# Attention scores and attention output: three fp32r passes in place of plain fp32 matmuls

## The chip, the cores and the metric

The kernel runs on one core of one Trainium2 chip. The number that counts is the device time of one execution in microseconds (us), as the median of several runs. A profiled execution shows what the core's engines did: PE (TensorE, matmuls; PEld is its loading of the stationary operand), DVE (VectorE), ACT (ScalarE), POOL (GpSimd) and SP (SyncE, which issues the DMAs).

## What is computed

One layer with two branches that read the same normalised input: an mLSTM branch and a latent attention branch (MLA). The change lies in the attention branch. There are 512 prompt tokens, and 64 new tokens of a second stream that has 128 cached keys; 8 heads, keys of 128 unrotated and 64 rotated columns, values of 128 columns.

```python
def mla_attend(qn, qr, q_pos, kn, kr, v, k_pos):
    s = (jnp.einsum('bqhd,bkhd->bhqk', qn, kn) + jnp.einsum('bqhd,bkd->bhqk', qr, kr)).astype(jnp.float32) * ATT_SCALE
    mask = (k_pos[None, :] // CHUNK) <= (q_pos[:, None] // CHUNK)
    s = jnp.where(mask[None, None], s, NEG)
    p = jax.nn.softmax(s, axis=-1).astype(v.dtype)
    return jnp.einsum('bhqk,bkhd->bqhd', p, v)
...
    q_nope = rmsnorm(q[..., :NOPE], g_qn)
    k_nope = rmsnorm(kv[..., :NOPE], g_kn)
    v = kv[..., NOPE:]
```

CHUNK is 64, so in a block of 128 queries that meets its own 128 keys, the first 64 queries may not see the last 64 keys. Everything is fp32.

## The kernel before

**Split products.** Most products in this kernel are made as three passes in the type fp32r: each operand is split into a rounded part (hi) and the rest (lo), and hi·hi, hi·lo and lo·hi are added up in PSUM. `split_of` makes the parts: a copy to hi on ACT, a subtraction for lo on DVE. `gemm_f` and `gemm_t` issue such products; `fblock` makes one 128-column block of an input projection for all 576 tokens (48 matmuls of 288 columns), with its weights loaded and split by `wload`.

**The attention stage** runs two heads (a pair) at a time. Its steps stand in the string `PLAN`: `K` makes queries, keys and values of a pair, `H` does one head, `Z` is the `fblock` of a head's gate, `G` the `fblock` of a merge gate that is needed at the end of the program (it is sent to DRAM), `P` the output projection of a pair. The stages follow one another as "G0 K0 Z0 H0 Z1 K1 H1 G2 G1 Z2 P0 H2 Z3 Z4 H3 ...".

- `K` (in `kq`): six `k_tile`s and five `q_tile`s, as generators, so that a tile's second half is issued after the first half of the second tile behind it. A `k_tile` makes 128 tokens' keys and values in PSUM, copies the keys to `kn` (DVE) and the values to `v` (ACT), takes the norm (ACT squares, DVE, POOL power of -0.5), scales `kn` on DVE, transposes it on PE and writes `kT` by ACT. A `q_tile` does alike for queries, with the rotation of the 64 rotary columns on POOL (lines 461 to 464).
- `H` (in `head`): scores of four query blocks against 128, 256, 384 and 512 keys and of the 64 sample tokens against 192. The unrotated part is a plain fp32 matmul (lines 529 and 536), the rotated part two fp32r matmuls (531, 538). The mask is a fourth matmul of one row, `indrow` by `negrow` (532), which adds -1e30 where a key is not to be seen. `soft` then takes maximum (510), exponential (511), reciprocal and scale. The probabilities are transposed on PE (547), copied to `pT` (548), and multiplied with `v` in plain fp32 (559, and 562, 563 for the sample tokens). The result multiplies the gate `za` (561, 564), and `split_of` makes the two parts `ha`.

A plain fp32 matmul shows in the trace as two MATMUL records.

**Buffers.** PSUM has three pools: `mm` with two banks (an `fblock` takes both), `sa` with three (scores, transposed probabilities, head outputs) and `sk` with three (K's tiles). In SBUF `qT` and `kT` have four buffers each, that is two pairs; `v` has two for pairs; the gate `za` has two; the tile `tg` of a `G` has one of its own.

**What sets the order.** The program is written in the order of `PLAN`. A scheduler then fixes, when the program is built, one order for each engine's queue: it goes by the order of the text, but takes a later instruction where an earlier one isn't ready by its own estimate, as long as a buffer is free for it. On the chip each engine works its queue off in that order and waits where an operand or a buffer is late.

Of the kernel before, what the change touches and what calls it, by code (L numbers as in the profile page):

```python
# [6 lines left out]
F32 = mybir.dt.float32  # L7
# [6 lines left out]
P = 128  # L14
# [13 lines left out]
# order in which the work of the first two stages is issued (see `steps` and the attention loop)  # L28
# [9 lines left out]
def layer(ctx: ExitStack, tc, A, O):  # L38
# [37 lines left out]
    negrow = const.tile([1, 64], BF16, name="negrow")  # L76
    dve.memset(negrow, NEG)
    indrow = const.tile([1, P], BF16, name="indrow")
    dve.memset(indrow, 0.0)
    dve.memset(indrow[:, 0:64], 1.0)  # L80
# [26 lines left out]
    def wload(srcs, nk, n, wp=None, unit=1024):  # L107
# [7 lines left out]
        hi = shp(wp.tile([P, unit], F32R, tag="whi", name="whi", bufs=2))  # L115
        lo = shp(wp.tile([P, unit], F32R, tag="wlo", name="wlo", bufs=2))
# [15 lines left out]
    def gemm_s(out, ws, x, t0):  # L132
        # 64 tokens: both parts of x, side by side in memory, are one stationary operand; fold() adds the results
# [54 lines left out]
    with ExitStack() as es:  # L188
# [151 lines left out]
        def gates():  # L340
            # log-sigmoid, running sums and maxima; rows are (chunk, head)
# [87 lines left out]
    with ExitStack() as es:  # L429
# [6 lines left out]
        def q_tile(wq, n, qT, qrT):  # L436
# [469 lines left out]
```

## Time and profile before

| | us |
|---|---|
| median of 3 runs | 825.41 |
| lowest, highest | 824.75, 825.55 |
| span of the profiled execution, first to last instruction | 822.5 |
| PE busy in the span | 810.0 |
| DVE busy | 478.7 |
| ACT busy | 362.0 |
| POOL busy | 141.4 |

The attention stage lies at about 60 to 370 us, the start ahead of it, the mLSTM heads and the output projection behind it. A busy time is the time in which an engine had some instruction under way. Matmuls overlap: the distance from one matmul's start to the next says what it costs the engine, and the duration of one record is longer than that.

### The profile page before, as it was taken

The page shows a single profiled execution, that of the slowest core. Times are in us where ns is not written, and L with a number is a line of the kernel's source. Part 1 is how long each engine was busy: PE and PEld are TensorE (multiplying, and loading weights), DVE is VectorE, ACT ScalarE, POOL GpSimd, SP SyncE. Part 2 cuts the span into 40 slices and gives each one's busy share as a digit, 9 for nine tenths or more (in the row PEclk, how much of TensorE's full clock was granted, in tenths as well). Part 3 has the DMA queues.
Part 4 walks back from the last instruction along what each step waited for, and adds up shares of the span by engine and source line. Part 5 has one row for each costly group of instructions (what it writes and reads, how often), then busy time and mean ns, then how long its engine had stood idle before and what let it go on. Part 6 is the DMA issues. An engine that isn't in the chain of part 4 may idle for free.

```text
span 822.5 us, 14924 instructions
## 1 busy us (share of the span) xinstructions
PE 810.0 (98%) x5759; PEld 761.5 (93%) x5759; DVE 478.7 (58%) x1211; ACT 362.0 (44%) x999; POOL 141.4 (17%) x253
## 2 busy tenths in 40 slices
PE   7899999999999999999999999999999999999998
PEld 6898997888898798889999999999999999999997
DVE  5666566755576658545534873775477355655431
ACT  5446556663555654322434544444454434332200
POOL 2343241410143133001001110110111011000000
PEclk9999999999999999999999999999999999999999
DMA  8431231013113011126223232333333432543332
GB/s 267 138 108 59 74 111 27 1 52 106 41 52 120 27 41 33 46 84 157 78 77 91 66 106 74 103 84 97 91 94 96 118 87 68 165 124 106 101 95 76
DMA packets 101742, 72.80 MB, mean 89 GB/s; under 512 B 5742, under 2 KB 95848, under 8 KB 101672
## 3 DMA queue, kind: packets, MB, share of 16 engines
q1 hardware_dynamic: 101672, 71.86, 30.5%
q8 instruction: 45, 0.74, 0.4%
q14 instruction: 25, 0.20, 0.1%
HBM read 64.24 MB, written 7.61 MB: 87 GB/s over the span
## 4 chain that ended last, share of the span: by engine, by line
PE 94%; DMA 3%; DVE 1%; ACT 1%; issue 0%; SPq 0%; POOL 0%; DVEq 0%; ACTq 0%
PE mm L126 58%; PE sk L143 10%; PE sk L852 3%; PE sa L852 3%; PE sa L529 2%; PE sa L728 2%; PE sa L559 2%; PE sk L728 2%; PE sk L136 2%; PE sa L531 1%; PE sa L547 1%; PE sk L745 1%; PE sa L136 1%; PE sk L502 1%; DMA part<-in_w_in 1%; DMA E<-gscr 1%
## 5 line engine op out<-in xcount | busy, mean ns | idle before, releaser
L105 DVE TENSOR_TENSOR wlo<-raw,whi 128x1024 fp32r<-128x1024 f32 (+1 forms) x88 | 108.5, 1234 | 92.1 <-ACT whi L104 87.1
L104 ACT CAST whi<-raw 128x1024 fp32r<-128x1024 f32 (+1 forms) x88 | 92.6, 1055 | 135.2 <-PE mm L126 91.9
L126 PE MATMUL mm<-hhi,whi 128*128 128x288 f32 x896 | 147.1, 300 | 1.1 <-ACT hhi L104 1.1
L126 PE MATMUL mm<-hhi,wlo 128*128 128x288 f32 x896 | 146.6, 299 | 0.0
L126 PE MATMUL mm<-hlo,whi 128*128 128x288 f32 x896 | 145.7, 298 | 0.0
L126 PEld LDWEIGHTS mm<-hhi,whi 128*128 128x128 f32 x896 | 126.6, 188 | 2.1 <-ACT hhi L104 1.4
L126 PEld LDWEIGHTS mm<-hlo,whi 128*128 128x128 f32 x896 | 127.1, 188 | 1.3 <-issue 0.5
L126 PEld LDWEIGHTS mm<-hhi,wlo 128*128 128x128 f32 x896 | 126.9, 188 | 1.2 <-issue 0.5
L74 POOL TENSOR_TENSOR r<-r,mhalf 128x2 f32<-128x2 f32 (+3 forms) x44 | 37.2, 844 | 165.4 <-DVE r L495 109.4
L126 PE MATMUL mm<-ha,whi 128*128 128x288 f32 x256 | 48.2, 307 | 0.6 <-DVE part L595 0.6
L126 PEld LDWEIGHTS mm<-ha,whi 128*128 128x128 f32 x256 | 37.3, 188 | 2.7 <-DVE part L595 1.1
L511 ACT ACTIVATE P<-sa,sc 128x128 f32<-128x128 f32 (+4 forms) x40 | 20.1, 503 | 36.4 <-DVE sc L510 35.6
L752 POOL TENSOR_TENSOR qi<-qf,wi 128x256 f32<-128x256 f32 (+1 forms) x16 | 11.9, 744 | 105.7 <-ACT qf L710 54.3
L595 DVE TENSOR_TENSOR part<-part,mm 128x288 f32<-128x288 f32 x48 | 21.4, 452 | 11.8 <-PE mm L126 11.6
L74 POOL TENSOR_TENSOR sc<-sc,mhalf 128x1 f32<-128x1 f32 (+1 forms) x20 | 13.0, 648 | 87.0 <-DVE sc L784 87.0
L126 PE MATMUL mm<-ha,wlo 128*128 128x288 f32 x128 | 27.5, 296 | 0.0
L105 POOL TENSOR_TENSOR qi<-qi,qi 128x256 fp32r<-128x256 f32 (+1 forms) x16 | 10.7, 668 | 85.3 <-ACT qi L104 85.3
L529 PE MATMUL sa<-kT,qT 128*128 128x128 f32 (+3 forms) x64 | 23.4, 447 | 0.0
L510 DVE TENSOR_REDUCE sc<-sa 128x1 f32<-128x128 f32 (+4 forms) x40 | 18.3, 457 | 8.5 <-PE sa L532 6.4
L728 PE MATMUL sk<-va,kw 128*128 128x258 f32 (+1 forms) x120 | 22.2, 290 | 0.1
L823 DVE SCALAR_TENSOR_TENSOR mt<-tgm,mm 128x288 f32<-128x288 f32 x16 | 7.3, 454 | 25.1 <-PE mm L126 25.1
L474 ACT ACTIVATE qT<-sk,gqn_c 128x128 f32<-128x128 f32 (+1 forms) x40 | 12.2, 354 | 18.8 <-PE sk L472 18.8
(353 smaller groups left out, 1641.0 us busy)
## 6 DMA issues: line engine op xcount, KB each, us to landing
raw<-in_w_in SPq DMA_DIRECT2D x56, 512.0 KB, 3.8
raw<-in_w_pa SPq DMA_DIRECT2D x8, 512.0 KB
raw<-in_w_pm SPq DMA_DIRECT2D x8, 512.0 KB, 4.2
raw<-in_w_uq SPq DMA_DIRECT2D x4, 576.0 KB, 4.0
gmscr<-tg SPq DMA_DIRECT2D x8, 288.0 KB
tgm<-gmscr SPq DMA_DIRECT2D x8, 288.0 KB, 4.3
xt<-in_x_prompt SPq DMA_DIRECT2D x4, 512.0 KB, 6.7
raw<-in_w_ukv SPq DMA_DIRECT2D x4, 512.0 KB, 3.8
```

What stands on the lines that cost most here:

```text
L74: pool.tensor_tensor(dst, ms, mhalf[0:n, 0:dst.shape[-1]], op=ALU.pow)
L104: act.copy(hi, src)
L105: (eng or dve).tensor_tensor(lo, src, hi.bitcast(F32), op=ALU.subtract)
L126: pe.matmul(ps[j], a[:, k0 + k, c0:c0 + P], b[:, k, sl], start=(n == 0), stop=(n == len(trip) - 1))
L136: pe.matmul(out, x[:, k, t0:t0 + P], a, start=(i == 0), stop=(i == len(trip) - 1))
L143: pe.matmul(out, b[:, k, t0:t0 + L], a[:, k, c0:c0 + n], start=(i == 0), stop=(i == len(trip) - 1))
L510: dve.tensor_reduce(sc[0:L, 0:1], ps, AX.X, ALU.max, negate=True)
L511: act.activation(pt[0:L, 0:n], ps, AF.Exp, bias=sc[0:L, 0:1], accum_out=sc[0:L, 1:2])
L529: pe.matmul(ps[:, 0:n], qT[hh][:, q0:q0 + P], kT[hh][:, 0:n], start=True, stop=False)
L595: dve.tensor_tensor(part[:, f, sl], part[:, f, sl], ps[j], op=ALU.add)
L728: pe.matmul(out, x, y, start=(first and i == 0), stop=(last and i == 2))
L852: pe.matmul(ps[0:L, 0:NB], x[:, 4 * u + k, t0:t0 + L], w[u][i][:, k], start=(q == 0), stop=(q == len(trip) - 1))
```

## The change

The scores' unrotated part and both products with `v` become three fp32r passes on split operands. For that queries, keys, values and transposed probabilities are stored as hi and lo parts: `scaled_split` scales from PSUM to hi on ACT and writes lo by one DVE operation. The mask matmul goes; a DVE memset writes -1e30 to 64 rows and 64 columns of the scores in PSUM. In `k_tile` the copy to `kn` goes: squares and scale (now on ACT) read PSUM, which is thus held until the scale is done. Buffers are per head, three for each of `qT`, `qrT`, `kT` and `v` (hi and lo), and the tile `tg` of a `G` now takes one of the two buffers of `za`. In `head` the output's PSUM bank `of` is taken ahead of the transposes, and the products with `v` follow each block of transposes rather than all of them. The scratch space of dynamic DMAs is set to 1024 bytes.

```diff
-    def wload(srcs, nk, n, wp=None, unit=1024):
+    def wload(srcs, nk, n, wp=None, unit=1024, tag="", bufs=2):
...
-                act.activation(qT[hh][:, t0:t0 + L], ps2[:, hh * P:hh * P + L], AF.Copy, scale=gqn_c)
-            dve.tensor_copy(qrT[:, :, t0:t0 + L], ps2.rearrange("p (k t) -> p k t", k=4)[:, 2:4, 0:L])
+                scaled_split(qT[hh], t0, L, ps2[:, hh * P:hh * P + L], gqn_c)
+                dve.tensor_copy(qrT[hh][:, t0:t0 + L], ps2[:, (2 + hh) * P:(2 + hh) * P + L])
...
+        def scaled_split(dst, t0, L, src, g):
+            hi, lo = (x[:, t0:t0 + L] for x in dst)
+            act.activation(hi, src, AF.Copy, scale=g)
+            dve.scalar_tensor_tensor(lo, src, g, hi.bitcast(F32), ALU.mult, ALU.subtract)
...
-                dve.tensor_copy(kn, pv[:, :, 0:NOPE])
-                act.copy(v[:, n], pv[:, :, NOPE:])
...
+            for hh in range(2):
+                split_of(v[hh][0:L, 0, n], v[hh][0:L, 1, n], pv[0:L, hh, NOPE:])
...
-                act.activation(sq[0:L], kn[0:L, hh], AF.Square, scale=NOPE ** -0.5, accum_out=r2[0:L, hh:hh + 1])
+                act.activation(sq[0:L], pv[0:L, hh, 0:NOPE], AF.Square, scale=NOPE ** -0.5, accum_out=r2[0:L, hh:hh + 1])
...
-                dve.tensor_scalar(kn[0:L, hh], kn[0:L, hh], r2[0:L, hh:hh + 1], None, ALU.mult)
+                act.activation(kn[0:L, hh], pv[0:L, hh, 0:NOPE], AF.Copy, scale=r2[0:L, hh:hh + 1])
...
-                act.activation(kT[hh][:, t0:t0 + L], ps2[:, hh * P:hh * P + L], AF.Copy, scale=gkn_c)
+                scaled_split(kT[hh], t0, L, ps2[:, hh * P:hh * P + L], gkn_c)
...
+        def scores(out, hh, qT, qrT, kT, qc, kc):
+            (qh, ql), (kh, kl) = qT[hh], kT[hh]
+            pairs = [(qh, kh), (qh, kl), (ql, kh), (qrT[hh], krhi), (qrT[hh], krlo)]
+            for i, (a, b) in enumerate(pairs):
+                pe.matmul(out, a[:, qc], b[:, kc], start=(i == 0), stop=(i == 4))
...
-                pe.matmul(ps[:, 0:n], qT[hh][:, q0:q0 + P], kT[hh][:, 0:n], start=True, stop=False)
-                for kr in (krhi, krlo):
-                    pe.matmul(ps[:, 0:n], qrT[:, hh, q0:q0 + P], kr[:, 0:n], start=False, stop=False)
-                pe.matmul(ps[:, n - 64:n], indrow, negrow, start=False, stop=True)
+                scores(ps[:, 0:n], hh, qT, qrT, kT, slice(q0, q0 + P), slice(0, n))
+                dve.memset(ps[0:64, n - 64:n], NEG)
...
+            of = SA()
...
-                (act.copy if j % 2 else dve.tensor_copy)(pT[:, o:o + w], ps[:, 0:w])
-                off.append(o)
-                o += w
+                pT = [aq.tile([P, 4 * P], F32R, tag=f"pT{x}", name=f"pT{x}", bufs=2)[:, 0:w] for x in range(2)]
+                split_of(pT[0], pT[1], ps[:, 0:w])
+                for i, (x, y) in enumerate(((0, 0), (0, 1), (1, 0))):
+                    pe.matmul(of[:, j * P:SEQ], v[:, x, j], pT[y], start=(j == 0 and i == 0), stop=(j == 3 and i == 2))
+            dve.tensor_tensor(za[:, 0:SEQ], of, za[:, 0:SEQ], op=ALU.mult)
...
-            qT = [aq.tile([P, T], F32, tag="qT", name="qT", bufs=4) for _ in range(2)]
-            qrT = aq.tile([P, 2, T], F32R, tag="qrT", name="qrT", bufs=2)
-            kT = [ak.tile([P, TK], F32, tag="kT", name="kT", bufs=4) for _ in range(2)]
-            v = ak.tile([P, 6, 2, VD], F32, tag="v", name="v", bufs=2)
...
+            qT = [[aq.tile([P, T], F32R, tag=f"qT{i}", name=f"qT{i}", bufs=3) for i in range(2)] for _ in range(2)]
+            qrT = [aq.tile([P, T], F32R, tag="qrT", name="qrT", bufs=3) for _ in range(2)]
+            kT = [[ak.tile([P, TK], F32R, tag=f"kT{i}", name=f"kT{i}", bufs=3) for i in range(2)] for _ in range(2)]
+            v = [ak.tile([P, 2, 6, VD], F32R, tag="v", name="v", bufs=3) for _ in range(2)]
...
-                gm_block(i, aq.tile([P, T], F32, tag="tg", name="tg", bufs=1))
+                gm_block(i, aq.tile([P, T], F32, tag="za", name="tg", bufs=2))
...
-    nc = _bacc.Bacc("TRN2", target_bir_lowering=False, num_devices=1)
+    nc = _bacc.Bacc("TRN2", target_bir_lowering=False, num_devices=1, dynamic_dma_scratch_size=1024)
```

How this moves instructions is seen at two places. A row names line, operation, output and inputs, and size; a number behind a name tells buffers of one name apart.

On ACT, during the first head (H0): L173 reads the results of the `fblock`s of G2 and G1 out of `mm`, and the rows of P_1404 and P_1415 are H0's first exponentials. Before:

```order
L511 ACTIVATE P_1404,sc<-sa,sc 128x128
L450 ACTIVATE sq,r_1252<-qs 128x128
L451 ACTIVATE sq,r_1252<-qs 128x64
L173 ACTIVATE tg<-mm 128x288
L511 ACTIVATE P_1415,sc<-sa,sc 128x256
L474 ACTIVATE qT<-sk,gqn_c 128x128 x2
L104 CAST whi<-raw 128x1024
L450 ACTIVATE sq,r_1291<-qs 64x128
L173 ACTIVATE tg<-mm 128x288
```

After, the first read of `mm` by a `tg` that follows G0's stands behind H0's last step, the split of `za` into `ha_1438`, and among the exponentials of the second head (P_2039 and on):

```order
L512 ACTIVATE P_2039,sc<-sa,sc 128x128
L99 CAST v<-sk 128x128 x3
L512 ACTIVATE P_2052,sc<-sa,sc 128x256
L99 CAST ha_1438<-za 128x576
L495 ACTIVATE sq,r_1663<-sk 128x128
L512 ACTIVATE P_2065,sc<-sa,sc 128x384
L495 ACTIVATE sq,r_1663<-sk 128x128
L495 ACTIVATE sq,r_1683<-sk 128x128
L168 ACTIVATE tg<-mm 128x288 x2
```

The read of G2's block has moved from H0's scores to a place behind H0.

On PE, in the third head (H2): transposes of the probabilities P (L547, after L549), `fblock` matmuls (L126) and the products with `v` (L559, after L553). Before:

```order
L547 MATMUL sa<-ident,P_2349 128x128
L547 MATMUL sa<-ident,P_2360 128x128 x2
L126 MATMUL mm<-hhi,wlo 128x288 x3
L552 MATMUL sa<-ident,P_2370 128x64
L553 MATMUL sa<-ident,P_2370 64x64
L126 MATMUL mm<-hhi,wlo 128x288 x3
L126 MATMUL mm<-hhi,whi 128x288 x8
L126 MATMUL mm<-hlo,whi 128x288 x8
L126 MATMUL mm<-hhi,wlo 128x288 x2
L559 MATMUL sa<-pT,v 128x512
L559 MATMUL sa<-pT,v 128x384
L559 MATMUL sa<-pT,v 128x256
```

After (pT_2551, pT_2562 are hi parts, pT_2552, pT_2563 lo parts):

```order
L549 MATMUL sa<-ident,P_2501 128x128
L549 MATMUL sa<-ident,P_2514 128x128
L549 MATMUL sa<-ident,P_2527 128x128
L553 MATMUL sa<-pT_2552,v 128x512
L553 MATMUL sa<-pT_2551,v 128x512
L549 MATMUL sa<-ident,P_2514 128x128
L549 MATMUL sa<-ident,P_2527 128x128
L553 MATMUL sa<-pT_2562,v 128x384
L553 MATMUL sa<-pT_2563,v 128x384
L553 MATMUL sa<-pT_2562,v 128x384
L553 MATMUL sa<-pT_2572,v 128x256
```

The `fblock` matmuls between transposes and products are gone from here; the products follow two transposes behind the block that they need.

## Rows read from the trace of the kernel before

**Rows 1.** The page: span, engines' busy time, and the granted PE clock by slices.

```profile
span 822.5 us, 14924 instructions
PE 810.0 (98%) x5759; PEld 761.5 (93%) x5759; DVE 478.7 (58%) x1211; ACT 362.0 (44%) x999; POOL 141.4 (17%) x253
...
PEclk9999999999999999999999999999999999999999
```

**Rows 2.** PE's longest wait: waited for, us in total, times, longest us.

```profile
PE sa L267 <- DVE xs L262: 2.7, 2, 1.4
```

**Rows 3.** Busy us (x instructions) of PE, PEld, DVE, ACT, POOL, clock; the attention stage.

```profile
60.00:370.00 310.00, 309.41 (x1954) 269.56 (x1954) 196.56 (x589) 162.19 (x582) 76.58 (x138) 1.00 0.20 58
```

**Rows 4.** The same for PE and PEld, L126 alone, in the first head.

```profile
104.00:125.00 21.00, 14.55 (x89) 12.02 (x87) 1.00 0.33 104
```

**Rows 5.** Timeline of PE between two heads: start us, us, engine, line, tiles, shapes.

```profile
276.37 2.42 PE L559 MATMUL sa<-pT,v 128*128 128x512 f32 x8
278.63 0.39 PE L529 MATMUL sa<-kT,qT 128*128 128x128 f32 x2
...
280.46 0.33 PE L562 MATMUL sa<-pTs,v 128*128 128x64 f32 x2
280.73 0.43 PE L563 MATMUL sa<-pTs,v 64*128 64x64 f32 x2
...
281.74 0.28 PE L531 MATMUL sa<-krlo,qrT 128*128 128x256 f32 x1
281.96 0.20 PE L532 MATMUL sa<-negrow,indrow 1*128 1x64 bf16 x1
...
285.09 0.20 PE L532 MATMUL sa<-negrow,indrow 1*128 1x64 bf16 x1
285.22 0.79 PE L143 MATMUL sk<-whi,cqhi 128*128 128x384 f32 x3
285.85 0.68 PE L143 MATMUL sk<-whi,cqlo 128*128 128x384 f32 x3
286.37 0.69 PE L143 MATMUL sk<-wlo,cqhi 128*128 128x384 f32 x3
```

**Rows 6.** The same timeline, two fp32r passes of 512 columns each.

```profile
263.49 0.62 PE L143 MATMUL sk<-whi,cklo 128*128 128x512 f32 x2
263.95 0.62 PE L143 MATMUL sk<-wlo,ckhi 128*128 128x512 f32 x2
```

**Rows 7.** Groups of PE instructions: xcount, busy us, mean ns, idle us: the mask matmuls.

```profile
L532 PE MATMUL sa<-negrow,indrow 1*128 1x64 bf16 x32 | 6.3, 198 | 0.0
```

**Rows 8.** Timeline of POOL: query tiles of the first pair, second to fifth.

```profile
100.59 1.01 POOL L74 TENSOR_TENSOR r<-r,mhalf 128x4 f32<-128x4 f32 x1 [3.95 <-DVE r L452]
...
110.57 1.01 POOL L74 TENSOR_TENSOR r<-r,mhalf 128x4 f32<-128x4 f32 x1 [0.48 <-DVE r L452]
...
113.47 0.46 POOL L464 TENSOR_TENSOR qr<-qr,rt 128x128 f32<-128x128 f32 x1
117.26 1.00 POOL L74 TENSOR_TENSOR r<-r,mhalf 64x4 f32<-64x4 f32 x1 [3.33 <-DVE r L452]
```

**Rows 9.** Groups of DVE and ACT instructions around the heads, as in rows 7.

```profile
L561 DVE TENSOR_TENSOR za<-sa,za 128x512 f32<-128x512 f32 x8 | 5.5, 690 | 10.0 <-PE sa L559 9.9
L510 DVE TENSOR_REDUCE sc<-sa 128x1 f32<-128x512 f32 x8 | 5.5, 687 | 5.0 <-PE sa L532 4.8
...
L513 DVE TENSOR_SCALAR P<-P,sc 128x384 f32<-128x384 f32 x8 | 3.3, 412 | 0.1
...
L510 DVE TENSOR_REDUCE sc<-sa 64x1 f32<-64x192 f32 x8 | 2.7, 343 | 1.7 <-PE sa L538 1.5
...
L564 DVE TENSOR_TENSOR za<-sa,za 128x64 f32<-128x64 f32 x8 | 1.7, 218 | 0.4 <-PE sa L563 0.4
...
L641 DVE MEMSET xp<- 128x3 f32 x8 | 0.5, 61 | 0.0
...
L511 ACT ACTIVATE P<-sa,sc 128x512 f32<-128x512 f32 x8 | 5.5, 688 | 14.1 <-DVE sc L510 14.1
```

More of the change, by code (lines that the diff above doesn't have):

```diff
@@ L74, in rsqrt_of @@
         pool.tensor_tensor(dst, ms, mhalf[0:n, 0:dst.shape[-1]], op=ALU.pow)
[L76 to L80, printed above, removed]
     cols = const.tile([P, 82], F32, name="cols")
@@ L114, in wload @@
             o += s.shape[0] // P
-        hi = shp(wp.tile([P, unit], F32R, tag="whi", name="whi", bufs=2))
-        lo = shp(wp.tile([P, unit], F32R, tag="wlo", name="wlo", bufs=2))
+        hi = shp(wp.tile([P, unit], F32R, tag="whi" + tag, name="whi", bufs=bufs))
+        lo = shp(wp.tile([P, unit], F32R, tag="wlo" + tag, name="wlo", bufs=bufs))
         split_of(hi, lo, raw)
@@ L522, in z_block @@
             return za
+        def scores(out, hh, qT, qrT, kT, qc, kc):
[3 more added lines that the diff above has]
+                pe.matmul(out, a[:, qc], b[:, kc], start=(i == 0), stop=(i == 4))
         def head(hh, qT, qrT, kT, v, za, ha):
+            v = v[hh]
             pts = []
@@ L535, in head @@
             nk = PAST + DEC
-            pe.matmul(ps[0:DEC, 0:nk], qT[hh][:, SEQ:T], kT[hh][:, SEQ:TK], start=True, stop=False)
-            for kr in (krhi, krlo):
-                pe.matmul(ps[0:DEC, 0:nk], qrT[:, hh, SEQ:T], kr[:, SEQ:TK], start=False, stop=(kr is krlo))
+            scores(ps[0:DEC, 0:nk], hh, qT, qrT, kT, slice(SEQ, T), slice(SEQ, TK))
             pt = soft(ps[0:DEC, 0:nk], DEC, nk)
-            pT = aq.tile([P, 10 * P], F32, tag="pT", name="pT", bufs=1)
-            off = []
-            o = 0
+            of = SA()
             for j in range(4):
@@ L553, in head @@
             pe.transpose(ps[0:DEC, 64:64 + DEC], pt[0:DEC, P:nk], ident[0:DEC, 0:DEC])
-            pTs = aq.tile([P, 2, DEC], F32, tag="pTs", name="pTs", bufs=1)
-            act.copy(pTs[:, 0], ps[:, 0:DEC])
-            act.copy(pTs[0:DEC, 1], ps[0:DEC, 64:64 + DEC])
-            of = SA()
-            for j in range(4):
-                pe.matmul(of[:, j * P:SEQ], v[:, j, hh], pT[:, off[j]:off[j] + (4 - j) * P],
-                          start=(j == 0), stop=(j == 3))
-            dve.tensor_tensor(za[:, 0:SEQ], of, za[:, 0:SEQ], op=ALU.mult)
-            pe.matmul(ps[:, 128:128 + DEC], v[:, 4, hh], pTs[:, 0], start=True, stop=False)
-            pe.matmul(ps[:, 128:128 + DEC], v[0:DEC, 5, hh], pTs[0:DEC, 1], start=False, stop=True)
+            pTs = [aq.tile([P, 2, DEC], F32R, tag=f"pTs{x}", name=f"pTs{x}", bufs=1) for x in range(2)]
+            split_of(pTs[0][:, 0], pTs[1][:, 0], ps[:, 0:DEC])
+            split_of(pTs[0][0:DEC, 1], pTs[1][0:DEC, 1], ps[0:DEC, 64:64 + DEC])
+            for c, L in ((0, P), (1, DEC)):
+                for i, (x, y) in enumerate(((0, 0), (0, 1), (1, 0))):
+                    pe.matmul(ps[:, 128:128 + DEC], v[0:L, x, 4 + c], pTs[y][0:L, c], start=(c == 0 and i == 0), stop=(c == 1 and i == 2))
             dve.tensor_tensor(za[:, SEQ:T], ps[:, 128:128 + DEC], za[:, SEQ:T], op=ALU.mult)
```

11 lines of the change are left out of this document (6 added, 5 removed).

## The prediction, made before the changed kernel ran

> **What bounds the kernel now.** I read the page's line of engines first: PE is busy for 810.0 of 822.5 us, the next engine, DVE, for 478.7, and PE's granted clock is at its upper level in every slice [rows 1]. Then the waits: PE's longest group of waits is 2.7 us in all, in one line of the start [rows 2]. Then the stretch in which everything that changes lies, 60 to 370 us: PE is busy in 309.41 of 310 us there, DVE in 196.56, ACT in 162.19, POOL in 76.58 [rows 3]. So PE sets the time and never waits in the attention stage; the other engines have room. The change is worth what it takes out of PE's queue, less the waits that it brings to PE. The median, 825.4, is 2.9 us above the span; I add that to what I reckon for the span.
>
> **The price of a pass.** Matmuls overlap, so I take the distance between starts. Two fp32r passes of 512 columns take 263.49 to 263.95, that is 0.23 us each [rows 6]; three of 384 take 285.85 to 286.37, 0.173 each [rows 5]. Both are 0.45 ns per column. The plain product with `v` has 1280 columns in four widths, two records for each, and takes 276.37 to 278.63, 2.26 us [rows 5], 0.88 ns per column and record, 1.77 for a product. Three passes cost 1.35 ns per column, a quarter less, as long as the columns set the price. For few columns they don't: two records of 64 columns take 280.46 to 280.73, 0.135 each, and the mask matmul of 64 columns takes 285.09 to 285.22, 0.13 [rows 5]. For a pass of 256 I take 0.12 (0.45 ns a column gives 0.115) and for one of 128 I take 0.11, near the short ones; its ends are 0.058 (by columns) and 0.135.
>
> **The change, part by part.**
>
> The mask matmul goes, 32 of them [rows 7]. Each costs its own 0.13. It also slows its neighbours: the 256-column pass ahead of it takes 281.74 to 281.96, 0.22 in place of 0.12, and the three 384-column passes behind another take 285.22 to 285.85, 0.63 in place of 0.52 [rows 5]. Together 0.13 + 0.10 + 0.10 = 0.33, times 32: **-10.6 us**. The end of that is -4.2 if the neighbours' part stays.
>
> The product with `v`: three passes cost 3 x (0.23 + 0.173 + 0.12 + 0.11) = 1.90 in place of 2.26, so -0.36 a head, **-2.8**. The scores' unrotated part has the same four widths and the same sum, **-2.8**; the 192 columns of the sample tokens come out even (0.33 against 0.34). The sample product with `v` goes from two records to three passes, twice: two such pairs take 0.27 + 0.36 = 0.63 [rows 5], so a third more is +0.21 a head, **+1.7**. With a 128-column pass at its ends the three together move between -6.4 and -2.7.
>
> PE's queue thus gets shorter by 10.6 + 2.8 + 2.8 - 1.7 = **14.5 us**, and nothing that hides another engine's work can take this back but a wait of PE.
>
> Waits of PE, and here the order counts more than the prices. Before, every chain of a head (maximum, exponential, scale, transpose, copy, product) ran beside `fblock` matmuls. In the first head these filled 14.55 of 21 us [rows 4]. After, `tg` needs a buffer of `za`, so G2's `fblock` cannot empty `mm` before H0 has given up its gate, and the second example of the order ahead shows the same in H2: the transposes and products stand back to back. Buffers of `qT`, `kT` and `v` for three heads, not four, hold the next pair's tiles back too.
>
> First head. Between the transposes of K0's second query tile and those of its fifth, the order after leaves PE 15 passes of 384, 12 of 512, some 19 transposes and the first head's scores: 2.6 + 2.8 + 2.1 + 3.2 = 10.7 us. The tiles' chain took 117.26 - 100.59 = 16.7 us in POOL's records before, with waits of POOL for DVE of 3 to 4 us among them [rows 8]. POOL's own part is at least 3.4 us a tile (110.57 to 113.93), 10 us for three. So PE waits between 0 and 6 us. I take 6, because the waits in that chain were for DVE, and DVE gets more to do: lo parts for queries, keys, values and probabilities.
>
> Heads with a dense stretch (H0 with H1's scores, H2 with H3's, H4 with H5's). Three places. The lo pass of the second block needs transposes, ACT's cast and DVE's subtraction (about half a microsecond each for 384 columns, by the 0.69 that 512 cost [rows 9]) and has 0.85 us of PE work between: wait 0.4. The second scores of the next head need the bank of `of`, which is free after DVE's multiplication, 0.69 [rows 9], with 0.55 of PE work between: 0.4 with the hand-over. The third transpose of the next head needs the 384-column probabilities, whose scale stands on DVE behind the maxima of the 512 and the 192 columns: from the end of the 512 scores 0.1 + 0.69 + 0.34 + 0.41 [rows 9] and four hand-overs, against 0.8 us of PE work (sample scores, two transposes): 1.4 with a tenth or two for each hand-over. With 0.3 for the rest it is 2.5 a stretch, 7.5 in all. H6 with H7's scores has some fill left, 1.3; the last head's products have little behind them, 1.2. Sum of the waits: 6 + 7.5 + 2.5 = **+16 us**; the ends are 6 (half of each, and nothing at the first head) and 24 (each stretch half as dear again).
>
> What DVE and ACT get on top: 32 memsets, each between 0.06 (a memset of 128x3) and 0.22 (a 128x64 operation with PSUM) [rows 9], I take 0.1 as it writes only; the second parts, 88 of them for queries and keys, at 0.3 to 0.5 us. That is some 30 us on DVE in a stage that leaves it 113 free [rows 3]; elsewhere PE's work covers it. If it didn't, that is the second rival. Three constants less at the start, single buffers for K's weights and the smaller DMA scratch: nothing, the weights are loaded a whole stage ahead, and PE's waits of the start are elsewhere [rows 2].
>
> A rule to be weighed against the pass prices: the Trainium skill, "TensorE: Matmul & The Clock Gate", section "Back-to-back issue gap", gives 131 ns per matmul of 512 columns in a stream and 81 ns for 128. This trace has 230 ns for 512 [rows 6], so I don't take it; by it a head's two sets of three passes would be about 1.25 us shorter (an estimate from that section's two figures), 10 in all, and the time would be 817.
>
> **Sum.** 822.5 + 2.9 - 14.5 + 16 = **827 us**, that is as before within what a measurement of this kernel can tell (0.2%, 1.65 us).
>
> **The rivals.**
>
> 1. *The waits are half of that.* The chains were slow because PE was the slow partner; with PE early, DVE and ACT are early too, and POOL's minimum (10 us) just fits the first head's 10.7. Waits of 8: 825.4 - 14.5 + 8 = 819. For it: POOL and ACT idle half of the stage [rows 3]. Against it: the waits of rows 8 are for DVE.
>
> 2. *DVE's queue becomes the bound in the other heads too* (H1, H3, H5, H7). There `fblock` matmuls remain, but memset, maximum, scale, subtraction and the splits of weights stand in one queue; from about 2 us of lateness per head the matmuls between are used up. Four times 2: 827 + 8 = 835, slower. For it: DVE goes from 63% of the stage to above 70%. Against it: its longest steps are 0.69 [rows 9].
>
> 3. *The clock falls.* In the emptier stretches PE pauses. If the granted clock falls to 1.2 GHz there, some 5 us of passes take twice their time: 832. In the trace before it is at its upper level in all slices, waits of 1.4 us included [rows 1, 2]. The Trainium skill, same page, section "HAM oscillation — how this bites in real kernels", says that idle gaps of PE let the clock fall again; no run here shows that yet.
>
> 4. *Wide passes overlap more when three share an accumulation.* If the passes of 512 and 384 columns cost half, 1.2 us a head more is saved, 9.7 in all: 817. The section on the issue gap named above points that way; rows 5 and 6 are against it, since those passes also accumulate.
>
> **How the numbers follow.** My forecast, pass prices as read and 11 to 21 us of waits, gets 0.45; its own range is 822 to 832, of which 0.08 is faster, 0.17 the same and 0.20 slower by over 0.2%. Rival 1 gets 0.29 (faster), rival 2 gets 0.16 (slower), rival 3 0.05 (slower), rival 4 0.05 (faster). Faster 0.42, same 0.17, slower 0.41. The range from 817 to 836 leaves out about 0.08 on either side.
>
> **What would show it.** The mask: no PE record of it, and passes next to where it stood at their plain distance. Passes: start distances of 0.23 for 512 columns in scores and products, about 0.11 for 128; three of 64 at 0.13. Waits: between about 100 and 125 us PE should wait for query tiles (transposes of `qs` and `q`) for some 6 us, and in each dense stretch for DVE at the lo products and for P at the third transpose. If PE's waits in the stage are under 8 us, rival 1 holds; if they stand in the odd heads beside `fblock` matmuls, rival 2; if a slice of the clock is below its upper level, rival 3. If wide passes start at less than 0.2, rival 4. What would make me wrong outright is a mask matmul that cost only its own 0.13: then the sum is 833.

## The result, and the profile after

| | before | after |
|---|---|---|
| median of the runs, us | 825.08 (4 runs, 824.52 to 825.55) | 849.44 (4 runs, 848.58 to 850.11) |
| ratio, with its 95% interval | | 1.0298 (1.0284 to 1.0313) |
| span of the profiled execution | 822.5 | 848.3 |
| PE busy | 810.0 | 815.8 |
| span less PE busy | 12.5 | 32.5 |
| lost in PE's busy time to a lower clock | 0 | 12.2 |

The change made the kernel slower by 24 us; 827 was forecast, with a range of 817 to 836. The last line of the table is worked out from windows of 1 us: the busy time of each, times what its granted clock lacks to 1. So PE's work at the upper clock is 815.8 - 12.2 = 803.6 us, 6.4 less than before, where 14.5 less were forecast. The span grew by 25.8 = 20.0 (idle) + 12.2 (clock) - 6.4 (work). The prediction had 16 - 14.5 = 1.5 for it, so it missed 24.3: 4.0 in the waits, 12.2 in the clock and 8.1 in the work.

The page of the changed kernel, the lines that answer to [rows 1]:

```profile
span 848.3 us, 15259 instructions
...
PE 815.8 (96%) x5815; PEld 777.9 (92%) x5815; DVE 507.2 (60%) x1352; ACT 387.9 (46%) x1091; POOL 138.4 (16%) x253
...
PEclk9999979999999999998999999999999999999999
```

The line of the clock has dents now, and PE is at 96%. The longest waits of PE (waited for, us in total, times, longest), in place of [rows 2]:

```profile
PE sa L529 <- ACT qT L475: 3.2, 4, 1.5
PE sk L467 <- DVE q L462: 2.5, 1, 2.5
PE mm L121 <- ACT tg L168: 2.4, 2, 1.9
PE sa L549 <- DVE P L514: 2.4, 2, 1.2
PE sa L262 <- DVE xs L257: 2.3, 2, 1.2
PE mm L121 <- DVE part L595: 1.5, 3, 0.6
```

L262 is the start, which both kernels have. The other five are new or longer and lie in the attention stage: scores that wait for queries, transposes that wait for the rotated queries and for probabilities, an `fblock` that waits for the tanh of the block before it, and output projections that wait for the sum of the pairs before (`part`). The windows of PE (stretch, length, PE busy and instructions, clock, DMA share, GB/s), the first head:

```profile
105.00:110.00 5.00, 3.97 (x28) 1.00 0.41 105
110.00:115.00 5.00, 3.55 (x14) 0.69 0.32 105
115.00:120.00 5.00, 2.27 (x13) 0.84 0.25 86
120.00:125.00 5.00, 3.71 (x10) 0.50 0.05 19
125.00:130.00 5.00, 5.00 (x15) 0.60 0.00 0
```

In the kernel before, PE was busy for all of 104 to 125 us, at the upper clock (the same columns):

```profile
104.00:125.00 21.00, 21.00 (x137) 1.00 0.33 104
```

Now it is busy in 13.5 of the 20 us from 105 to 125, and its clock falls to 0.50, the lower of its levels (1.2 GHz). At 125 to 130 us PE waits for nothing any more and is still slow. The timeline of PE shows both losses (start, us, line, tiles, shape; in brackets the idle time ahead and what ended it):

```profile
108.70 0.27 PE L466 MATMUL sk<-ident,qs 128*128 128x128 f32 x1
110.50 0.44 PE L529 MATMUL sa<-kT,qT 128*128 128x128 f32 x2 [1.53 <-ACT qT L475]
111.89 0.47 PE L529 MATMUL sa<-kT,qT 128*128 128x128 f32 x1 [0.95 <-DVE qT L476]
...
115.84 0.28 PE L529 MATMUL sa<-krlo,qrT 128*128 128x256 f32 x1
118.62 0.40 PE L467 MATMUL sk<-ident,q 128*128 128x128 f32 x1 [2.50 <-DVE q L462]
...
125.88 0.63 PE L529 MATMUL sa<-krhi,qrT 128*128 128x512 f32 x1
126.31 0.63 PE L529 MATMUL sa<-krlo,qrT 128*128 128x512 f32 x1
```

1.53 + 0.95 us go for the hi and the lo part of the first query tile, 2.50 for the rotated queries of a later one. From 125.88 to 126.31 a pass of 512 columns takes 0.43 us in place of the 0.23 of [rows 6]: the same pass at half the clock.

### The profile page after: what moved, and what is told of

It reads as the page before. It is cut to its first block, busy times and chain, and to the rows that moved or that the text cites. A ratio compares the mean times of both kernels' runs of the same rounds, so it can differ in the third digit from the quotient of the medians.

```text
span 848.3 us, 15259 instructions
## 1 busy us (share of the span) xinstructions
PE 815.8 (96%) x5815; PEld 777.9 (92%) x5815; DVE 507.2 (60%) x1352; ACT 387.9 (46%) x1091; POOL 138.4 (16%) x253
## 4 chain that ended last, share of the span: by engine, by line
PE 87%; DVE 5%; DMA 4%; ACT 3%; issue 1%; SPq 0%; DVEq 0%; ACTq 0%
PE mm L121 56%; PE sk L138 8%; PE sa L852 3%; PE sk L852 3%; PE sa L728 2%; PE sa L529 2%; DMA raw<-in_w_in 2%; PE sk L728 2%; PE sa L553 2%; DVE wlo L100 1%; PE sk L131 1%; PE sk L745 1%; DMA rif<-in_w_in 1%; PE sa L131 1%; PE sa L549 1%
## 5 line engine op out<-in xcount | busy, mean ns | idle before, releaser
L121 PE MATMUL mm<-hhi,wlo 128*128 128x288 f32 x896 | 144.6, 298 | 0.0
L121 PE MATMUL mm<-hlo,whi 128*128 128x288 f32 x896 | 143.3, 297 | 0.0
L529 PE MATMUL sa<-kT,qT 128*128 128x128 f32 (+4 forms) x120 | 29.8, 337 | 5.4 <-ACT qT L475 3.2
L121 PE MATMUL mm<-ha,wlo 128*128 128x288 f32 x128 | 28.2, 302 | 0.0
L595 DVE TENSOR_TENSOR part<-part,mm 128x288 f32<-128x288 f32 x48 | 21.4, 450 | 11.3 <-PE mm L121 11.2
L529 PEld LDWEIGHTS sa<-kT,qT 128*128 128x128 f32 (+1 forms) x120 | 19.2, 186 | 8.7 <-ACT qT L475 4.1
L553 PE MATMUL sa<-pT,v 128*128 128x512 f32 (+3 forms) x96 | 25.0, 346 | 1.0 <-ACT pT L99 0.4
L100 DVE TENSOR_TENSOR pT<-sa,pT 128x512 fp32r<-128x512 f32 (+3 forms) x32 | 15.6, 490 | 16.6 <-ACT pT L99 16.3
```

The lines of the kernel that those rows point to most:

```text
L100: (eng or dve).tensor_tensor(lo, src, hi.bitcast(F32), op=ALU.subtract)
L121: pe.matmul(ps[j], a[:, k0 + k, c0:c0 + P], b[:, k, sl], start=(n == 0), stop=(n == len(trip) - 1))
L529: pe.matmul(out, a[:, qc], b[:, kc], start=(i == 0), stop=(i == 4))
L553: pe.matmul(of[:, j * P:SEQ], v[:, x, j], pT[y], start=(j == 0 and i == 0), stop=(j == 3 and i == 2))
L595: dve.tensor_tensor(part[:, f, sl], part[:, f, sl], ps[j], op=ALU.add)
```

## The experiments

Times are medians in us; the ratio is to runs of the kernel before taken beside them, with its 95% interval. The kernel before gave 823.8 beside e1 to e4, 825.0 beside e5 to e8 and 825.3 beside e9 and e10, so results are compared by their ratios, times 825. "Idle" is span less PE busy, "clock" the loss worked out as above; both are of the one profiled execution, and the clock differs between executions of one kernel. The mean granted clock of the four executions of e3 was 0.985 to 0.993 and of e9 0.982 to 0.992, and in both the profiled one had the lowest clock and the longest time; the five of e10 had 0.995 to 1.000, and the profiled one had 1.000.

| run | median | ratio (interval) | PE busy | idle | clock |
|---|---|---|---|---|---|
| e1 memset | 817.7 | 0.9925 (0.9909 to 0.9940) | 800.7 | 15.0 | 0 |
| e2 tg in za | 837.8 | 1.0164 (1.0142 to 1.0187) | 817.7 | 18.6 | 5.9 |
| e3 own tg | 842.7 | 1.0229 (1.0206 to 1.0251) | 814.1 | 28.8 | 11.3 |
| e4 busy PE | 845.8 | 1.0268 (1.0252 to 1.0285) | 815.7 | 27.8 | 4.9 |
| e5 products3 | 824.7 | 1.0002 (0.9983 to 1.0020) | 805.5 | 16.7 | 1.7 |
| e6 scores3 | 820.4 | 0.9951 (0.9936 to 0.9965) | 800.8 | 17.4 | 0 |
| e7 three heads | 824.4 | 0.9995 (0.9986 to 1.0005) | 804.9 | 16.2 | 1.7 |
| e8 k holds PSUM | 828.5 | 1.0053 (1.0032 to 1.0074) | 806.9 | 19.6 | 3.3 |
| e9 own tg, kn | 842.0 | 1.0193 (1.0176 to 1.0210) | 814.8 | 28.2 | 12.7 |
| e10 plain products | 829.6 | 1.0059 (1.0038 to 1.0081) | 802.4 | 24.6 | 0 |

### e1: the mask alone

```diff
...
-                    pe.matmul(ps[:, 0:n], qrT[:, hh, q0:q0 + P], kr[:, 0:n], start=False, stop=False)
-                pe.matmul(ps[:, n - 64:n], indrow, negrow, start=False, stop=True)
+                    pe.matmul(ps[:, 0:n], qrT[:, hh, q0:q0 + P], kr[:, 0:n], start=False, stop=(kr is krlo))
+                dve.memset(ps[0:64, n - 64:n], NEG)
```

> The kernel before with one part of the change alone: the mask matmul and its two constants are gone, a DVE memset writes -1e30 into the scores. If the mask matmul costs itself and its neighbours, 0.33 us each for 32, this is 825.1 - 10.6 = 814.5 us. If only its own 0.13 counts, 821. If the memset delays the softmax and PE waits for it, 825 or more.

817.7 us, 0.75% faster than the kernel before: between the first and the second figure. PE's busy time fell by 810.0 - 800.7 = 9.3 us, not far from the 10.6; idle time rose by 2.5, of which 1.0 lies ahead of 60 us, where the edit has no part. The pass ahead of the place of the mask is short again (timeline of e1):

```profile
110.81 0.28 PE L526 MATMUL sa<-krlo,qrT 128*128 128x256 f32 x1
110.93 0.96 PE L121 MATMUL mm<-hhi,whi 128*128 128x288 f32 x6
...
124.05 0.39 PE L526 MATMUL sa<-krlo,qrT 128*128 128x512 f32 x1
124.28 0.62 PE L138 MATMUL sk<-whi,ckhi 128*128 128x512 f32 x2
124.75 0.62 PE L138 MATMUL sk<-whi,cklo 128*128 128x512 f32 x2
```

256 columns take 0.12 where [rows 5] had 0.22 ahead of a mask, and two passes of 512 behind its place take 0.47. The memset that does the work costs DVE 0.112 us (group of e1: mean ns 112), against 0.1 taken in the prediction:

```profile
L527 DVE MEMSET sa<- 64x64 f32 x32 | 3.6, 112 | 4.9 <-PE sa L526 4.6
```

e1 beats both kernels and is the version to keep.

### e2: the gate's buffer alone

```diff
-                gm_block(i, aq.tile([P, T], F32, tag="tg", name="tg", bufs=1))
+                gm_block(i, aq.tile([P, T], F32, tag="za", name="tg", bufs=2))
```

> The kernel before with one part of the change alone: tg of a G takes one of the two buffers of za. Theory: this sharing alone takes the fblock matmuls out of the first head's stretch, so PE waits there for the query tiles (6 us or more) and the granted clock falls to its lower level for about 10 us: 835 to 845 us, with a slice of the clock below its upper level. Rival: plain fp32 products keep PE busy enough and the chains short enough; the sharing costs under 3 us, and the waits of the changed kernel come from the split operands: 825 to 828.

837.8: this one line, with plain products and the mask matmul, costs 13.5 us, more than half of what the whole change cost. The windows of PE in e2:

```profile
105.00:110.00 5.00, 3.61 (x22) 1.00 0.30 104
110.00:115.00 5.00, 3.72 (x10) 0.55 0.29 105
115.00:120.00 5.00, 4.09 (x8) 0.50 0.00 0
```

The `fblock` matmuls are gone from there, PE waits, and the clock falls, without any split operand in scores or products. Of the 5.9 us that the clock takes, 4.2 lie here and 1.7 at 373 to 377 us. The rival is out for this part of the loss.

### e3: the changed kernel with tg in a buffer of its own

```diff
-                gm_block(i, aq.tile([P, T], F32, tag="za", name="tg", bufs=2))
+                gm_block(i, aq.tile([P, T], F32, tag="tg", name="tg", bufs=1))
...
-            q2 = ap.tile([P, 2, 2, ROPE], F32R, tag="q2", name="q2", bufs=1)
+            q2 = ap.tile([P, 2, 2, ROPE], F32R, tag="kn", name="q2", bufs=2)
...
-            pTs = [aq.tile([P, 2, DEC], F32R, tag=f"pTs{x}", name=f"pTs{x}", bufs=1) for x in range(2)]
+            pTs = [aq.tile([P, 4 * P], F32R, tag=f"pT{x}", name=f"pTs{x}", bufs=2)[:, 0:2 * DEC].rearrange("p (c t) -> p c t", c=2) for x in range(2)]
```

> The changed kernel with tg in a buffer of its own again (room for it comes from q2 taking a buffer of kn, and pTs one of pT). Theory: the fblock matmuls come back beside the first head, and with them the clock: about 12 us of waits and clock in 105 to 130 us go, 849.4 - 12 = 837 us; the second head, which then has no fblock beside it, may take some of it back. Rival: the waits come from the split operands' chains on ACT and DVE wherever they stand: 846 to 850, with the waits moved to the second head.

842.7, or 1.0229 against 1.0298: 5.7 us had back of the 12 expected. The first head has its fill and its clock again (idle time of 0.7 us in 100 to 130 us, none lost to the clock). Of the 11.3 us that the profiled execution loses to the clock, 4.7 are new, at 144 to 152 and at 209 to 214 us; 1.7 at 73 to 77 and 4.8 at 370 to 384 us stand about where the changed kernel loses too. The time lies between the theory (837) and the rival (846 to 850): the first head is cured, and about half of what that gave is lost again further on.

### e4: more work for PE in the first head

```diff
         def scores(out, hh, qT, qrT, kT, qc, kc):
...
+            for _ in range(spare[0]):
+                pe.matmul(out, qh[:, qc], kh[:, kc], start=True, stop=True)
...
+                spare[0] = 8 if i == 0 else 0
                 head(i % 2, *tens[i // 2], zas[i], has[i // 2])
```

> The changed kernel with 40 more passes in the first head alone: eight ahead of each of its five score blocks, overwritten by the real ones, 5.9 us of PE work at the upper clock. Theory: the clock falls because PE pauses there; with PE kept busy the clock stays at its upper level in 110 to 130 us, the passes there take half as long (5 to 7 us saved), and the added passes run mostly in time in which PE waited: 844 to 849 us in spite of more work. Rival: the lower clock costs nothing because PE waits for other engines there anyway: the time rises by the added work, 852 to 856.

845.8 against 849.4: 40 more matmuls, and the kernel is faster by about 2.5 us by the ratios (the intervals of the two just touch, 1.0252 to 1.0285 and 1.0284 to 1.0313). The windows of PE in e4, beside those of the changed kernel above:

```profile
105.00:110.00 5.00, 4.46 (x31) 1.00 0.25 74
110.00:115.00 5.00, 3.71 (x26) 1.00 0.31 105
115.00:120.00 5.00, 4.00 (x15) 0.66 0.33 105
120.00:125.00 5.00, 4.54 (x23) 1.00 0.01 3
125.00:130.00 5.00, 4.59 (x31) 1.00 0.00 0
```

The clock is at its upper level in all but 116 to 120 us. PE's queue is the same in both kernels but for the 40 passes (and one transpose that stands a few places later), so the same instructions can be compared. The last transpose ahead of the first head's scores, and two of the transposes of its probabilities, in e4:

```profile
107.54 0.27 PE L466 MATMUL sk<-ident,qs 128*128 128x128 f32 x1
132.75 0.38 PE L551 MATMUL sa<-ident,P 128*128 128x128 f32 x2
```

In the changed kernel they start at 108.70 and 135.52. So e4 is 1.16 us ahead at the first place and 2.77 at the second: with 6.1 us of PE work more between them it takes 1.6 us less, for 3.35 of idle time and 4.4 of clock are had back there. So the lower clock does cost time and is not only a sign of waiting, and in this stretch PE's pauses bring it: work that nobody needs keeps it up.

The rest of e4's gain lies where both kernels run the same instructions, and most of it is the clock too. At 71 us PE waits 1.93 us in both; the clock is low behind it in the changed kernel and not in e4. The timeline of PE, the changed kernel first, then e4:

```profile
73.22 1.35 PE L121 MATMUL mm<-hhi,whi 128*128 128x288 f32 x8 [1.93 <-ACT tg L168]
```

```profile
73.55 1.32 PE L121 MATMUL mm<-hhi,whi 128*128 128x288 f32 x8 [1.93 <-ACT tg L168]
```

The windows of PE behind it, in the same order:

```profile
74.00:78.00 4.00, 4.00 (x21) 0.57 0.19 74
```

```profile
74.00:78.00 4.00, 4.00 (x31) 1.00 0.21 78
```

The same holds of the waits ahead of 238 us; e4 in turn has a fall at 10 to 15 us, at the start, that the changed kernel hasn't. One wait of 2 us is thus followed by a lower clock in one execution and not in another. Only the 1.6 us in the first head can be put down to the 40 passes.

### e5 to e8: one part each on top of e1

e5, the products in three passes; all transposes stay ahead of the products, `pT` and `v` get a second part:

```diff
-                (act.copy if j % 2 else dve.tensor_copy)(pT[:, o:o + w], ps[:, 0:w])
+                split_of(pT[0][:, o:o + w], pT[1][:, o:o + w], ps[:, 0:w])
...
-                pe.matmul(of[:, j * P:SEQ], v[:, j, hh], pT[:, off[j]:off[j] + (4 - j) * P],
-                          start=(j == 0), stop=(j == 3))
+                for i, (x, y) in enumerate(((0, 0), (0, 1), (1, 0))):
+                    pe.matmul(of[:, j * P:SEQ], v[:, x, j, hh], pT[y][:, off[j]:off[j] + (4 - j) * P],
+                              start=(j == 0 and i == 0), stop=(j == 3 and i == 2))
```

> e1 (the mask by a memset) with one part more: the product with v as three fp32r passes on split operands, all transposes ahead of the products as in the kernel before, tg in a buffer of its own, four heads' queries and keys. Theory: with fblock matmuls beside it the passes cost what the rows say, 1.1 us less than e1: 816 to 818 us. Rival: the splits of v and of the probabilities on ACT and DVE make PE wait also here: 820 to 826.

824.7, 6.4 us above e1 by the ratios: the rival. Room for the second parts was made as in the changed kernel (single buffers for K's weights, small DMA scratch) and by giving `q2` a buffer of `kn`; these stand in the result too. The passes themselves cost what was reckoned: the products of the prompt take 15.5 us from start to start in all heads together (8 x 1.90 = 15.2 in the prediction), 17.0 in e1. The loss is elsewhere. The span is 6.5 us longer than e1's: 1.7 are idle time, 1.7 a lower clock at 358 to 362 us and 3.1 work, of which the sample products make 1.6 (1.7 reckoned). PE waits, as in the changed kernel, for a tanh at the first pair, and for split probabilities and for keys:

```profile
PE mm L121 <- ACT tg L168: 1.8, 1, 1.8
...
PE sa L557 <- DVE pT L100: 0.5, 1, 0.5
PE sk L138 <- ACT kT L501: 0.5, 1, 0.5
```

e6, the scores in three passes, with three buffers each for `qT` and `kT` (hi and lo) and all else as in e1:

```diff
-                pe.matmul(ps[:, 0:n], qT[hh][:, q0:q0 + P], kT[hh][:, 0:n], start=True, stop=False)
+                for i, (a, b) in enumerate(((0, 0), (0, 1), (1, 0))):
+                    pe.matmul(ps[:, 0:n], qT[hh][a][:, q0:q0 + P], kT[hh][b][:, 0:n], start=(i == 0), stop=False)
...
-                act.activation(kT[hh][:, t0:t0 + L], ps2[:, hh * P:hh * P + L], AF.Copy, scale=gkn_c)
+                scaled_split(kT[hh], t0, L, ps2[:, hh * P:hh * P + L], gkn_c)
```

> e1 with one part more: the scores as three fp32r passes on split operands, with buffers of qT and kT for three heads and not four; tg in a buffer of its own, products with v plain. Theory: the passes save 2.8 us, the three buffers hold back the next pair, whose tiles were fill: 815 to 822. Rival: the second parts of queries and keys lengthen the tile chains so that PE waits in the first head: 825 or more, with a low clock.

820.4, within the theory's span, 2.1 us above e1: PE's busy time is the same as in e1 to 0.1 us, so the 2.8 us of the passes were not had, and 2.4 us of idle time came on top. The scores with their rotated part take 30.8 us from start to start, 30.3 in e1. The clock stays up. (e6 and e8 have the small DMA scratch of the changed kernel too.)

e7, buffers for three heads, one head each, nothing else:

```diff
-            qT = [aq.tile([P, T], F32, tag="qT", name="qT", bufs=4) for _ in range(2)]
...
-            v = ak.tile([P, 6, 2, VD], F32, tag="v", name="v", bufs=2)
+            qT = [aq.tile([P, T], F32, tag="qT", name="qT", bufs=3) for _ in range(2)]
...
+            v = [ak.tile([P, 6, VD], F32, tag="v", name="v", bufs=3) for _ in range(2)]
```

(and `qrT`, `kT` alike)

> e1 with buffers of qT, kT, qrT and v for three heads each, per head, and nothing else: plain products, tg in a buffer of its own. Theory: the next pair's tiles are held back and the odd heads lose fill, but fblock matmuls are left: up to 4 us more than e1, 818 to 822. Rival: this buffering takes as much as the sharing of za did (14 us), then 830 or more.

824.4, 5.8 us above e1: more than the theory's 4, far from the rival. In the profiled execution (824.0) 1.7 us are a lower clock at 12 to 16 us, ahead of anything that the edit touches; but of the ten executions the one with a clock of 1.000 took 823.5, so the clock explains about 1 of the 5.8.

e8, the key tile as in the changed kernel, without the copy to `kn`:

```diff
-                dve.tensor_copy(kn, pv[:, :, 0:NOPE])
...
-                act.activation(sq[0:L], kn[0:L, hh], AF.Square, scale=NOPE ** -0.5, accum_out=r2[0:L, hh:hh + 1])
+                act.activation(sq[0:L], pv[0:L, hh, 0:NOPE], AF.Square, scale=NOPE ** -0.5, accum_out=r2[0:L, hh:hh + 1])
...
-                dve.tensor_scalar(kn[0:L, hh], kn[0:L, hh], r2[0:L, hh:hh + 1], None, ALU.mult)
+                act.activation(kn[0:L, hh], pv[0:L, hh, 0:NOPE], AF.Copy, scale=r2[0:L, hh:hh + 1])
```

> e1 with the key tile as in the changed kernel and nothing else: no copy to kn, squares and scale by ACT out of PSUM, the bank held until then. Theory: PE gets a bank for its next tile later, and waits once at the first pair, where the changed kernel waited 1.9 us at 71 us for a tanh and then ran at the lower clock for 3.4 us: about 4 us more than e1, 821 to 823. Rival: no wait, 817 to 818.

828.5, 10.6 us above e1, more than twice the theory. An edit that saves a DVE copy for each tile, moves the scale from DVE to ACT and adds nothing to PE turned 6 us of gain into 4 of loss. The span is 10.8 us longer than e1's: 4.6 idle time, 3.3 clock and 2.9 work. The wait that the changed kernel has at 71 us is here, and the clock behind it (timeline, then windows of PE in e8):

```profile
70.48 0.38 PE L498 MATMUL sk<-ident,kn 128*128 128x128 f32 x2
72.74 2.29 PE L121 MATMUL mm<-hhi,whi 128*128 128x288 f32 x8 [1.88 <-ACT tg L168]
```

```profile
70.00:72.00 2.00, 0.86 (x6) 1.00 0.03 8
72.00:74.00 2.00, 1.26 (x5) 0.69 0.07 28
74.00:76.00 2.00, 2.00 (x10) 0.50 0.32 120
```

In the kernel before PE has the next key tile's passes at that time. Here the banks are held until the keys are scaled, PE has only the `fblock`, and that waits for a tanh. Eight `fblock` matmuls take 2.29 us, nearly twice the 1.22 that they take at the upper clock. That place explains 1.9 us of waiting and 1.6 of clock. Holding the bank for the scale is not the only thing that brings the wait: e5 keeps the copy to `kn` and splits `v` out of PSUM, and has it too (1.84 us at 71 us), with the clock at 1.00 behind it.

### e9 and e10: parts of the changed kernel undone together

e9 is e3 with the copy to `kn` back:

```diff
+                dve.tensor_copy(kn, pv[:, :, 0:NOPE])
...
-                act.activation(sq[0:L], pv[0:L, hh, 0:NOPE], AF.Square, scale=NOPE ** -0.5, accum_out=r2[0:L, hh:hh + 1])
+                act.activation(sq[0:L], kn[0:L, hh], AF.Square, scale=NOPE ** -0.5, accum_out=r2[0:L, hh:hh + 1])
...
-                act.activation(kn[0:L, hh], pv[0:L, hh, 0:NOPE], AF.Copy, scale=r2[0:L, hh:hh + 1])
+                dve.tensor_scalar(kn[0:L, hh], kn[0:L, hh], r2[0:L, hh:hh + 1], None, ALU.mult)
```

> e3 (the changed kernel with tg in a buffer of its own) with the copy to kn back in the key tile, squares and scale from kn, so that the bank is free after the copy. Theory: what the key tile cost alone in e8, 828.5 - 817.7 = 10.8 us, is had back here: 842.7 - 10.8 = 832 us. Rival: with the other lengthened chains the fill is missing anyway, and the key tile is no longer what ends last: 838 to 843.

842.0: about 3 us had back by the ratios, not 10.8; the intervals of e3 and e9 just overlap, so even the 3 are not certain. The time is the rival's: parts that cost 2 to 14 us each where they stand alone don't add, and taking one away moves the pauses rather than ending them. In the profiled execution the clock falls at 126 to 134 and 229 to 237 us now (6.2 us lost), at 369 to 383 as in e3 (4.8), and at the start (1.7).

e10 is e9 with plain products, interleaved with the transposes as in the changed kernel:

```diff
-                split_of(pT[0], pT[1], ps[:, 0:w])
-                for i, (x, y) in enumerate(((0, 0), (0, 1), (1, 0))):
-                    pe.matmul(of[:, j * P:SEQ], v[:, x, j], pT[y], start=(j == 0 and i == 0), stop=(j == 3 and i == 2))
...
+                (act.copy if j % 2 else dve.tensor_copy)(pT, ps[:, 0:w])
+                pe.matmul(of[:, j * P:SEQ], v[:, j], pT, start=(j == 0), stop=(j == 3))
```

> e9 with the products with v in plain fp32 again (one copy of the probabilities for each block, v in one part); scores in three passes, three heads' buffers. Theory: what the split products cost alone in e5, 824.7 - 817.7 = 7 us, is had back: 7 us below e9, 825 if e9 is at 832; this should then be near e6 and e7 together (817.7 + 2.7 + 6.7 = 827, if these add). Rival: the passes are cheaper than the plain products here and their chains hidden: at e9's time or above.

829.6, 11 us below e9, where 7 were expected, and near the 827 that e6 and e7 add up to. In the two profiled executions the span differs by 16.0 us, and 12.7 of it are the clock: it takes nothing in e10, which still has 24.6 us of idle time. So pauses don't always bring the clock down; it stays at 1.00 even where PE is idle for a third of the time:

```profile
125.00:130.00 5.00, 3.96 (x20) 1.00 0.35 101
...
143.00:148.00 5.00, 3.29 (x16) 1.00 0.00 0
```

This is one execution. Two of e10's five had a mean clock of 0.995 and 0.996, and they took 831.9 and 832.8 us, the longest of the five.

The work at the upper clock is the same in e9 and e10 (802.1 and 802.4 us): plain products that are interleaved with the transposes cost PE as much as split ones there.

## Why the prediction was wrong, point by point

**What bounds the kernel: right.** PE is busy for 96% of the span or more in every run. But the prediction went on from there to say that nothing but a wait of PE can take back what its queue is shorter by. Two other things did: the clock, 12.2 us, and work that did not get shorter as reckoned, 8.1 us (1.3 at the mask, 6.8 at the passes).

**The mask: nearly right.** -10.6 forecast, -9.3 of PE's busy time in e1, -6.2 of the whole, with 2.5 us of idle time that the edit brought only in part. The price of its neighbours, taken from two places of [rows 5], was the right idea; over 32 places PE's share came to 0.29 each, not 0.33.

**The passes: this step failed.** Three passes for a plain product were to save 3.9 us in all. The changed kernel has 803.6 us of work at the upper clock and e1 has 800.7: PE has 2.9 more, so the step was off by 6.8 us. Not all of that is the passes' own: e7 and e8, with plain products throughout, have 803.2 and 803.6. Summed from start to start, three terms show what was mis-sized:

- The products with `v`, -2.8 forecast: 17.0 us plain in e1, 15.5 in e5, so -1.5. The pass price was right (15.2 reckoned); the plain price, 2.26 a head, was read at one place, and the mean is 2.13. In the changed kernel they take 19.5 and in e10, interleaved alike but plain, 19.1. So the 2 us and more on top go with the new place of the products, between the transposes, and not with the passes.
- The scores, -2.8 forecast: 30.3 us in e1 and 30.8 in e6, both with the rotated part, so nothing was saved. The prediction took the price of the plain scores over from the products ("the same four widths and the same sum") and read no row of the scores for it.
- The sample products, +1.7 forecast: 5.1 in e1, 6.7 in e5, so +1.6: right.

What was missed besides is that a pass whose operand is a little late may show no wait. The products of the first head (timeline of the changed kernel):

```profile
135.52 0.38 PE L549 MATMUL sa<-ident,P 128*128 128x128 f32 x2
135.78 0.44 PE L553 MATMUL sa<-pT,v 128*128 128x384 f32 x1
136.38 0.73 PE L553 MATMUL sa<-pT,v 128*128 128x384 f32 x3
...
137.64 0.69 PE L553 MATMUL sa<-pT,v 128*128 128x128 f32 x3
138.17 0.50 PE L529 MATMUL sa<-kT,qT 128*128 128x128 f32 x3
```

From the hi pass of 384 columns to the lo pass it is 0.60 us, where a pass costs 0.17: the 0.4 us of waiting for ACT's cast and DVE's subtraction that the prediction put there. But the first record lasts 0.44 us, so that most of the delay lies under it and counts as busy time; the row has no bracket. Three passes of 128 columns take 0.53 in place of 0.33. All products of the prompt together take 4 us more than in e5, where the transposes stand ahead. Such stalls come on top of the idle time below. What they make in the scores and transposes of the changed kernel was not taken apart.

**The waits: right in kind, too small.** +16 forecast, +20.0 of idle time measured, and the hidden stalls beside it. In the first head 6 us were forecast, and PE is idle for 6.5 of 105 to 125 us, but that is in part luck: 2.7 of it are the transposes of `qs` and `q` that the forecast named, nearly all the rest are scores that wait for the parts of the queries (1.53 + 0.95 + 0.35 + 0.82), which it did not name. In the dense stretches the third transpose waits 1.21 us for P at 221 and at 301 us (1.4 forecast), and the second scores 0.23 for the bank of `of` (0.4 forecast): right in place and kind. The wait of 1.9 us at 71 us was not foreseen: the held bank of the key tile had been named in the change's description, and no price was put on it. e8, which has this part of the change alone, is 10.6 us above e1.

**The clock: the step that failed most.** It was the third rival, 5 us with a chance of 0.05; the sum has nothing for it, and it took 12.2 us (74 to 78, 111 to 116, 118 to 129, 238 to 242 and 381 to 389 us). The error was to conclude from [rows 1, 2], one execution, that pauses of 1.4 us leave the clock alone. The same execution of the kernel before is idle for half of a stretch at its start, and keeps the upper clock (columns as above):

```profile
7.00:12.00 5.00, 2.50 (x14) 1.00 1.06 382
```

but e4, e7 and e9 lose 1.6 to 1.7 us to the clock in the same start. So a row of a single execution could not tell what a pause costs; e4's wait at 71 us says the same. What the runs do show is a matter of the dense case: in the first head of the changed kernel PE is idle for a third of 20 us, and the clock is at its lower level for most of 111 to 129 us; e4 fills that stretch with work, and 4.4 us of the loss there are had back. The Trainium skill, "TensorE: Matmul & The Clock Gate", section "HAM oscillation — how this bites in real kernels", has it that PE's idle gaps let the clock fall and that the work behind them then runs slowly; the first head agrees, with 0.50 at 120 to 125 us and a pass of 0.43 in place of 0.23. e10 keeps 1.00 at 143 to 148 us, where PE is idle for a third of the time too, so what decides it stays open.

**The buffer tg: the right place, and dearer than thought.** That G2's `fblock` would be missing beside the first head was read from the order, and e2 shows that this line alone costs 13.5 us, nearly half of it in the clock (5.9). e3 shows that its cure alone does not help much.

**The rivals.** Rival 1 (shorter waits) and rival 4 (cheaper wide passes) are out: idle time grew by 20.0 us, not 8, and the median pass of 512 columns still costs 0.23. Rival 2 gave the nearest time (835) for a cause that did not show: idle time stands at the dense stretches and the first pair, and DVE is busy for 60% of the span.

**What stays open.** Why a part costs 6 to 14 us alone (e2, e5, e7, e8; with e6 some 38 in all) and all of them together only 31 (the changed kernel against e1) was seen, not explained: each edit makes the scheduler write another order for the whole stage, and the effect of an edit and that of the order it happens to give were not separated.

## What to carry to other kernels

Where one engine is busy for 98%, a change that cuts its work is judged by what fills its queue while others are late: read from the order which independent work stood beside a chain, and whether a buffer taken away removes it. If pauses gather, count the clock as a price of its own, half the speed for the work that follows, and look at more than one execution before saying that it stays up. Read the price of each plain product from a row of its own. Make the parts of a change one by one: here one of them (the mask) was worth 6 us, and each of the others took time back.

## What the runs showed that had not been expected

- Forty matmuls that compute nothing made the stretch in which they stand shorter by 1.6 us, since they kept the clock up (e4). The whole kernel got faster by 2.5 us (ratios); the rest lies outside that stretch.
- The idle time of 24.6 us in e10's profiled execution cost no clock, 18.6 us in e2's cost 5.9: the sum of the pauses doesn't tell what the clock takes.
- The same queue with the same wait of 1.93 us ran at 0.57 behind it in one execution and at 1.00 in another (the changed kernel and e4, 74 to 78 us).
- A matmul's late operand hides under the record of the matmul ahead (0.44 us long for a pass that costs 0.17), so that stalls of some 0.3 us a pass count as PE's busy time.
- A DVE memset of 64x64 in PSUM takes 0.112 us; the matmul that it replaced took 0.29 us of PE.
